# Seven products over all eight feature tiles in the second network's up projection

## The chip, the core and the metric

The kernel runs on one core of a Trainium2 chip. Its engines work side by side, each through its own fixed list of instructions: TensorE (PE, matmuls, with weight loads shown as PEld), VectorE (DVE), ScalarE (ACT), GpSimd (POOL) and SyncE (SP). Here POOL does nothing but issue DMAs, and SP issues most of the others. Matmuls write to PSUM, everything else lies in SBUF. An instruction waits on semaphores until its inputs are written and its output buffer is free, and everything behind it on the same engine waits too. The metric is the device time of one execution in microseconds.

## The reference, cut to what matters

A two-layer backbone (a state-space mixer, then differential attention), each layer followed by a gated convolutional network on 640 tokens (512 latent, 128 context), width 1024. The change touches that network, for the most part that of the second layer:

```python
def conv_ffn(h, up_w, conv_w, conv_b, down_w):
    u = dwconv(h @ up_w, conv_w, conv_b)
    a, v = jnp.split(u, 2, axis=-1)
    return (jax.nn.silu(a) * v) @ down_w
...
xs = xs + s_g2 * conv_ffn(modulate(xs, norm_ffn_g[i], s_sh2, s_sc2), *ffn_p)
```

`up_w` is 1024 x 5632, `down_w` is 2816 x 1024. All is float32.

## The kernel before, in words

**Precision.** Each operand of a large matmul is split into a high part (rounded by an ACT copy to the format that TensorE reads, `fp32r`) and a low part (what is left). A product is three matmuls: high x high, high weight x low data, low weight x high data (`block`, line 652; `dense_many`, line 184). `cast` (line 134) makes both parts of a weight: ACT the high part, DVE the low part by a subtraction (line 171). For weights in `self.summed` (line 1380) the low part is made otherwise (lines 167 and 168): ACT writes the negated high part, and a DMA issued by POOL adds the original weight from DRAM onto it.

**Weights.** `weight_units` (line 1343) lists all weights in order. `prefetch` loads them into four `raw` buffers, `cast` into high and low buffers: a pool `w` of three and, in the networks, a pool `x` of two, chosen by the unit's number (line 143). A new weight takes the buffer of the one that many places back in its pool, so its cast waits until PE is done with that one.

**The network** (`ffn`, line 627). The hidden width is 22 tiles of 128. A "pair" p is the gate tile p and the value tile p, each a 128-row slice of the up product. `epilogue` (line 639) turns a pair into a gated tile: convolution of both halves (`conv`: one ACT step, then steps on DVE), SiLU on ACT, product on DVE, then its high part `mh` (ACT) and low part `ml` (DVE). After a portion of the pairs, `project_out` (line 308) multiplies their gated tiles with the down weights: eight output tiles, each added to the residual by three DVE operations (`gate_add`). `SUB` gives three portions of 8, 7 and 7 pairs; one more pair than the portion holds is done before its projection. `start_tiles` (line 342) does the first three up tiles in two halves of the tokens, the first half while the second half of `h` is still being normalised.

**Seven products.** From pair `S0[l]` on (16 in the first network, 4 in the second) four of the eight feature tiles are handled as a 2 x 2 block product: rows are the gate and the value weights, the inner dimension two groups of `NS` = 2 feature tiles, columns the two halves of the tokens (320 each). `pair7` (line 701) forms it by seven block products instead of eight, with sums of weights (`s12`, `s34`, made by DVE in `cast`) and sums of data (`T1` to `T4`, made once by `operands`, line 663, in a round per feature tile while earlier pairs run). The other four feature tiles (`rest`) are multiplied in the ordinary way, 4 x 4 weight tiles.

**Order.** The program is written in one sequence; a scheduler places each engine's instructions by priority and its own estimate of time, and that order is then fixed for each engine.

Of the kernel before, what the change touches and what calls it, by code (L numbers as in the profile page):

```python
# [18 lines left out]
P = 128  # L19
# [29 lines left out]
class Step:  # L49


    def __init__(self, ctx, tc, a):
        self.ctx, self.tc, self.nc, self.a = ctx, tc, tc.nc, a
        self.tasks = []
        self.ticks = 0
        self.wi = 0
        self.normt = {}
        self.ready = []
        self.px = None
        self.modtask = None  # L60
        self.late = []
        self.down = False
        self.wraw, self.wcast = {}, {}
        self.units = []
# [57 lines left out]
    def prefetch(self, upto):  # L122
        while len(self.wraw) <= min(upto, len(self.units) - 1):
            u = len(self.wraw)
            ap, n = self.units[u]
            if ap is None:
                self.wraw[u] = None
                continue
            r = self.pw.tile([P, 1024], F32, tag="raw", name=f"raw{u}", bufs=RAW)
            dst = r[:, :n]  # L130
            self.nc.sync.dma_start(dst.rearrange("p (i c) -> p i c", i=ap.shape[1]) if len(ap.shape) == 3 else dst, ap)
            self.wraw[u] = r

    def cast(self, upto):
        while len(self.wcast) <= min(upto, len(self.units) - 1):
# [1 line left out]
            self.prefetch(u)  # L137
            n = self.units[u][1]
            r = self.wraw[u]
            sums = self.units[u][0] is None  # L140
            c0 = 2 * NS * P if u and self.units[u - 1][0] is None else 0
            wp, t, b = (self.pw, "w", 3) if self.px is None or u % 5 < 3 else (self.px, "x", 2)
            hi = wp.tile([P, 1024], F32R, tag=t + "hi", name=f"whi{u}", bufs=b)
            lo = wp.tile([P, 1024], F32R, tag=t + "lo", name=f"wlo{u}", bufs=b) if u else None
            if u == 0:
# [4 lines left out]
            elif sums:  # L150
                self.prefetch(u + 1)
                ra, rv = self.wraw[u - 1], self.wraw[u + 1]
                w = NS * P
                s12, s34 = (self.slot("f", nm, bufs=NF) for nm in ("s12", "s34"))
                self.tt(s12[:, :w], rv[:, :w], rv[:, w:2 * w], ALU.add)
                self.tt(s12[:, w:2 * w], s12[:, :w], ra[:, :w], ALU.subtract)
                self.tt(s34[:, :w], ra[:, :w], rv[:, :w], ALU.subtract)
                self.tt(s34[:, w:2 * w], ra[:, w:2 * w], s12[:, w:2 * w], ALU.subtract)
                for j, s in enumerate((s12, s34)):
                    c = slice(2 * w * j, 2 * w * (j + 1))  # L160
                    self.act(hi[:, c], s[:, :2 * w], AF.Copy)
                    self.tt(lo[:, c], s[:, :2 * w], hi[:, c].bitcast(F32), ALU.subtract)
            else:
                c = slice(c0 // 2, n)
# [462 lines left out]
    def ffn(self, l, h, nextnorm, pool):  # L627
# [11 lines left out]
        def epilogue(p, ua, uv):  # L639
# [6 lines left out]
            hi = self.slot("mh", f"mh{p}", F32R, bufs=9, pool=pool)  # L646
            lo = self.slot("ml", f"ml{p}", F32R, bufs=9, pool=pool)
            self.act(hi, cv, AF.Copy)
            self.tt(lo, cv, hi.bitcast(F32), ALU.subtract)
            mid[p] = (hi, lo)  # L650

        def block(ps, w, c0, xs, first, last, more=False):

            hi, lo = w
            for i, (xh, xl) in enumerate(xs):
# [4 lines left out]
                if i % 2:  # L660
                    self.hook()

        def operands(out):

            cut = lambda t, j: t[:, j * TH:(j + 1) * TH]
            B = [[[tuple(cut(t, j) for t in h[NS * k + i]) for i in range(NS)] for j in range(2)] for k in range(2)]
            Ts = [[], [], [], []]
            for i in range(NS):
                f1, f2 = self.tmp("f1"), self.tmp("f2")
                for f, k in ((f1, i), (f2, NS + i)):  # L670
# [7 lines left out]
                yield 4  # L678
                if l:
                    hi, lo = (pool.tile([P, 3 * TH], F32R, tag=f"T{nm}{i}", name=f"T{nm}{i}", bufs=1) for nm in "hl")  # L680
                elif i:
                    both = pool.tile([P, 2, 3 * TH], F32R, tag="cbc", name=f"T{i}", bufs=1)
                    hi, lo = both[:, 0, :], both[:, 1, :]
                else:
                    hi, lo = (pool.tile([P, 3 * TH], F32R, tag="mw", name=f"T{nm}{i}", bufs=2) for nm in "hl")
                t3 = self.slot("f", f"T3_{i}", F32R, bufs=NF)
                for o, x in ((slice(0, T), t12), (slice(T, T + TH), cut(t43, 0))):
# [3 lines left out]
                self.act(cut(t3, 0), cut(t43, 1), AF.Copy)  # L691
                self.tt(cut(t3, 1), cut(t43, 1), cut(t3, 0).bitcast(F32), ALU.subtract)
                Ts[0].append((cut(hi, 0), cut(lo, 0)))
                Ts[1].append((cut(hi, 1), cut(lo, 1)))
                Ts[2].append((cut(t3, 0), cut(t3, 1)))
                Ts[3].append((cut(hi, 2), cut(lo, 2)))
                yield 3
            rest = [[tuple(cut(t, j) for t in h[k]) for k in range(2 * NS, KT)] for j in range(2)]
            out.extend((B, Ts, rest))

        def pair7(p, B, Ts, rest):


            (B11, _), (B21, B22) = B
# [1 line left out]
            u = self.wi  # L706
            self.wi += 3
            self.prefetch(u + 6)
            self.cast(u + 3 if l else u + 2)
            wa, ws, wv = (self.wcast[u + j] for j in range(3))  # L710
            w, r0 = NS * P, 2 * NS * P
            ua, uv = (self.slot("f", "uraw", bufs=NF) for _ in range(2))
            p5 = self.slot("f", "p5", bufs=NF)[:, :TH]
            lft, rgt = slice(0, TH), slice(TH, T)
            ps = self.dense_ps("up")
            X, Y = ps[:, :TH], ps[:, 512:512 + TH]
            block(X, wa, 0, B11, True, True)
# [26 lines left out]
                self.act(uv[:, lft], X, AF.Copy)  # L744
            epilogue(p, ua, uv)

        def pair(p):
            if p >= S0[l]:
                self.drain(self.seven)
                return pair7(p, *sevens)  # L750
# [5 lines left out]
        sevens = []  # L756
        self.seven = self.add(operands(sevens), 8) if l else None
        for s, (k0, k1) in enumerate(SUB):
            self.down = False
            while done < min(k1 + 1, FT):  # L760
                pair(done)
# [5 lines left out]
            if s == len(SUB) - 1 and self.modtask:  # L767
                self.drain(self.modtask)
            if s < len(SUB) - 1:
# [573 lines left out]
    def weight_units(self):  # L1343
# [9 lines left out]
        def ffn(l):  # L1353
            done = 0
            out = []
            for k0, k1 in SUB:
                while done < min(k1 + 1, FT):
                    sums = [(None, 1024)] if done >= S0[l] else []
                    out.extend([(a["w_up"][l, done], 1024), *sums, (a["w_up"][l, FT + done], 1024)])
                    done += 1  # L1360
                out.extend([(a["w_dn"][l, i, :, k0 * P:k1 * P], (k1 - k0) * P) for i in range(KT)])
            return out

        u += ffn(0)
# [8 lines left out]
        u += ffn(1)  # L1373
        return u
# [138 lines left out]
```

## Time and profile before

| | |
|---|---|
| median of 3 runs | 1866.02 us (1863.74 to 1867.49) |
| profiled execution | 1866.73 us, of which the span from first to last instruction is 1865.0 |
| mean granted TensorE clock | 0.994 |
| second network | from about 1391 us to the end |
| its first seven-product pair (pair 4) | at 1449.5 us |

A page of the profile gives busy times per engine, the chain of work that ended last (followed back from the last instruction to what released each step), and groups of equal instructions. In a group's row, `out<-in` names what is written and read; behind the bar stand the busy time and the mean duration, then the idle time of the engine just before these instructions and what ended it. A timeline row gives start and duration in us. Instructions on DVE and ACT overlap a little, so the distance from start to start is shorter than the duration.

### The profile page before, as it was taken

Reading aid. Unit: us, or ns where it says so; the run is one execution under the profiler, and the core shown is the slowest. Engines: PE = TensorE matmul, PEld = TensorE weight load, DVE = VectorE, ACT = ScalarE, POOL = GpSimd, SP = SyncE. Lnnn points to the kernel's source line nnn. Section 1 sums busy time; section 2 is a strip of 40 time slices with the busy share of each in tenths; the row PEclk is TensorE's granted clock in tenths of the full one; section 3 lists DMA queues with packets and bytes.
Section 4 is the critical chain, followed back from the end, with each engine's and each line's share of the span. In section 5 each row is a group of like instructions: output and inputs, shape, how many; then the busy total and the mean of one; then the engine's idle time right before and its main releaser. Section 6 shows DMA issues by size and latency. Waiting matters only on the chain.

```text
span 1865.0 us, 33040 instructions
## 1 busy us (share of the span) xinstructions
PE 1822.6 (98%) x13178; PEld 1720.5 (92%) x13178; DVE 1447.5 (78%) x2877; ACT 1005.3 (54%) x1889; POOL 31.7 (2%) x40
## 2 busy tenths in 40 slices
PE   7999999999999999999999999999999999999997
PEld 5899999989999999999999988888899999999996
DVE  5689999999758999986685878778878772772774
ACT  3489687878336441442453556567547642652751
POOL 0000000000000000000000000000000000100100
PEclk9999999999999999999999999999999999999998
DMA  9845343436533556532131211111122552653531
GB/s 333 262 133 141 100 151 100 134 123 198 185 113 117 193 178 220 190 111 74 50 110 61 89 51 64 59 42 51 53 100 59 130 141 66 160 138 79 138 98 57
DMA packets 84866, 226.28 MB, mean 121 GB/s; under 512 B 9852, under 2 KB 16616, under 8 KB 84584
## 3 DMA queue, kind: packets, MB, share of 16 engines
q1 hardware_dynamic: 78952, 207.13, 34.2%
q0 software_dynamic: 5184, 16.52, 5.0%
q8 instruction: 103, 1.69, 0.4%
q10 hardware_dynamic: 576, 0.52, 0.1%
q14 instruction: 51, 0.42, 0.1%
HBM read 218.18 MB, written 5.96 MB: 120 GB/s over the span
## 4 chain that ended last, share of the span: by engine, by line
PE 88%; DVE 5%; ACT 3%; DMA 2%; issue 1%; SPq 0%; DVEq 0%; ACTq 0%
PE up L107 30%; PE po L107 25%; PE z L107 6%; PE x L107 5%; PE st L107 5%; PE bc L107 3%; PE yp L107 3%; PE q L107 2%; PE k L107 1%; PE modrow L107 1%; PE sl L107 1%; PE in L107 1%; ACT whi L98 1%; ACT e L98 1%; PE ov L107 1%
## 5 line engine op out<-in xcount | busy, mean ns | idle before, releaser
L98 ACT ACTIVATE whi<-raw 128x1024 fp32r<-128x1024 f32 (+3 forms) x227 | 228.5, 1008 | 297.3 <-PE po L107 175.5
L104 DVE TENSOR_TENSOR wlo<-raw,whi 128x1024 fp32r<-128x1024 f32 (+2 forms) x190 | 224.2, 1181 | 46.5 <-ACT whi L98 41.3
L101 DVE SCALAR_TENSOR_TENSOR xr<-po,mod,xr 128x256 f32<-128x256 f32 (+2 forms) x231 | 89.6, 435 | 149.9 <-PE po L107 149.7
L107 PE MATMUL po<-mh,whi 128*128 128x256 f32 (+1 forms) x704 | 168.1, 310 | 0.1
L107 PE MATMUL po<-ml,whi 128*128 128x256 f32 (+1 forms) x704 | 167.6, 310 | 0.0
L107 PE MATMUL po<-mh,wlo 128*128 128x256 f32 (+1 forms) x704 | 167.2, 309 | 0.0
L107 PE MATMUL up<-h01h,whi 128*128 128x256 f32 (+1 forms) x596 | 147.2, 310 | 0.1
L107 PE MATMUL up<-h01l,whi 128*128 128x256 f32 (+1 forms) x596 | 146.3, 308 | 0.0
L107 PE MATMUL up<-h01h,wlo 128*128 128x256 f32 (+1 forms) x596 | 145.7, 308 | 0.0
L107 PE MATMUL up<-h11h,whi 128*128 128x320 f32 (+1 forms) x476 | 141.6, 313 | 1.5 <-ACT uraw L98 1.2
L107 PE MATMUL up<-h11l,whi 128*128 128x320 f32 (+1 forms) x476 | 140.1, 308 | 0.0
L107 PE MATMUL up<-h11h,wlo 128*128 128x320 f32 (+1 forms) x476 | 137.9, 308 | 0.0
L107 PEld LDWEIGHTS po<-mh,whi 128*128 128x128 f32 x704 | 128.4, 188 | 0.8 <-ACT mh L98 0.5
L107 PEld LDWEIGHTS po<-ml,whi 128*128 128x128 f32 x704 | 128.5, 188 | 0.2 <-DVE ml L104 0.2
L107 PEld LDWEIGHTS po<-mh,wlo 128*128 128x128 f32 x704 | 128.5, 188 | 0.0
L107 PEld LDWEIGHTS up<-h01h,whi 128*128 128x128 f32 x596 | 109.1, 188 | 1.7 <-ACT uraw L98 1.2
L107 PEld LDWEIGHTS up<-h01l,whi 128*128 128x128 f32 x596 | 109.2, 188 | 0.0
L107 PEld LDWEIGHTS up<-h01h,wlo 128*128 128x128 f32 x596 | 109.0, 188 | 0.0
L101 DVE SCALAR_TENSOR_TENSOR cv<-uraw,fcw,cv 128x511 f32<-128x511 f32 (+1 forms) x176 | 86.8, 549 | 24.1 <-ACT cv L98 23.9
L107 PEld LDWEIGHTS up<-h11h,whi 128*128 128x128 f32 x476 | 88.7, 188 | 5.2 <-ACT uraw L98 2.9
L101 DVE SCALAR_TENSOR_TENSOR ca<-uraw,fcw,ca 128x511 f32<-128x511 f32 (+1 forms) x176 | 90.4, 550 | 2.8 <-ACT ca L98 2.0
L107 PEld LDWEIGHTS up<-h11l,whi 128*128 128x128 f32 x476 | 88.9, 188 | 0.0
(527 smaller groups left out, 4845.3 us busy)
## 6 DMA issues: line engine op xcount, KB each, us to landing
raw<-in_w_up SPq DMA_DIRECT2D x88, 512.0 KB, 3.7
mw<-in_modT SPq DMA_DIRECT2D x48, 512.0 KB, 4.0
raw<-in_w_in SPq DMA_DIRECT2D x40, 512.0 KB, 5.3
rb<-rowd SPq DMA_DIRECT2D x40, 512.0 KB, 5.6
raw<-in_w_dn SPq DMA_DIRECT2D x32, 448.0 KB, 3.3
raw<-in_w_qkv SPq DMA_DIRECT2D x24, 512.0 KB, 3.3
mr<-in_mod SPq DMA_DIRECT2D x44, 256.0 KB, 5.3
wlo<-in_w_up POOLq DMA_DIRECT2D x18, 512.0 KB, 7.2
```

Of the source, the lines that this page charges most:

```text
L98: return self.nc.scalar.activation(out, in_, func, **k)
L101: return self.nc.vector.scalar_tensor_tensor(out, in0, s, in1, op0, op1)
L104: return self.nc.vector.tensor_tensor(out, a, b, op)
L107: return self.nc.tensor.matmul(out, lhsT, rhs, start=start, stop=stop, skip_group_check=more)
```

## The change

In the second network the 2 x 2 block product covers all eight feature tiles: `NS` becomes 2 and 4, so a pair there is seven block products of four feature tiles and no rest. The pair has four weight units (gate, `s12`, `s34`, value); the gate always takes pool `x`, the other three pool `w`. The new `pair8` and `begin7` run a pair, the first product of the next pair ahead of the last of this one. `operands` makes four rounds there; the data of `T4` overwrite the second half of the first four tiles of `h`, in `finish_operands`, when pair 4 is reached. The down projection has five portions (4, 4, 4, 4 and 6 pairs), with six buffers for gated tiles in place of nine. The low parts of the gated tiles, all but the last, are made by a negated ACT copy and an accumulating DMA from POOL's queue (a copy within SBUF), and the low parts of all 44 up weights of the second network by such a DMA, where before it was those of pairs 4 and after. In the first network the sums of weights are cast one by one, and `T4` is finished last.

```diff
-SUB = ((0, 8), (8, 15), (15, 22))
+SUB = ((0, 8), (8, 15), (15, 22)), ((0, 4), (4, 8), (8, 12), (12, 16), (16, 22))
+MIDS = 9, 6
-NS = 2
+NS = 2, 4
...
-            sums = self.units[u][0] is None
-            c0 = 2 * NS * P if u and self.units[u - 1][0] is None else 0
-            wp, t, b = (self.pw, "w", 3) if self.px is None or u % 5 < 3 else (self.px, "x", 2)
+            kind = self.units[u][2]
+            place = self.units[u][3] or ("x" if self.px and u % 5 > 2 else "w")
+            wp, t, b = (self.pw, "w", 3) if place == "w" else (self.px, "x", 2)
...
+            elif isinstance(kind, tuple):
+                ns, j0, ia, iv = kind
+                self.prefetch(u + iv)
+                ra, rv = self.wraw[u + ia], self.wraw[u + iv]
+                w = ns * P
+                for j in range(j0, j0 + 1024 // w):
+                    x = self.slot("f", f"s{j}", bufs=NF)[:, :w]
+                    a, b, op = ((rv[:, :w], rv[:, w:2 * w], ALU.add), (self.s.get(0), ra[:, :w], ALU.subtract),
+                                (ra[:, :w], rv[:, :w], ALU.subtract), (ra[:, w:2 * w], self.s.get(1), ALU.subtract))[j]
+                    self.tt(x, a, b, op)
+                    self.s[j] = x
+                    c = slice(w * (j - j0), w * (j - j0 + 1))
+                    self.act(hi[:, c], x, AF.Copy)
+                    self.tt(lo[:, c], x, hi[:, c].bitcast(F32), ALU.subtract)
...
             self.act(hi, cv, AF.Copy)
-            self.tt(lo, cv, hi.bitcast(F32), ALU.subtract)
+            if l and p < FT - 1:
+                self.act(lo, cv, AF.Copy, scale=-1.0)
+                nc.gpsimd.dma_start(lo, cv, accum_op=ALU.add)
+            else:
+                self.tt(lo, cv, hi.bitcast(F32), ALU.subtract)
...
                 if l:
                     hi, lo = (pool.tile([P, 3 * TH], F32R, tag=f"T{nm}{i}", name=f"T{nm}{i}", bufs=1) for nm in "hl")
+                    x4 = tuple(cut(t, 1) for t in h[i])
+                    late.append((x4, cut(t43, 0)))
+                    parts = (slice(0, T), t12), (slice(T, T + TH), cut(t43, 1))
...
+        def begin7(p):
+            u = self.wi
+            self.wi += 4
+            self.prefetch(u + 7)
+            self.cast(u + 2)
+            ua, uv = (self.slot("f", "uraw", bufs=NF) for _ in range(2))
+            if self.nps % 2:
+                Y, X, V = bank(), bank(), bank()
+            else:
+                X, V, Y = bank(), bank(), bank()
+            (B11, _), _ = sevens[0]
+            block(X, self.wcast[u], 0, B11, True, True)
+            with self.tc.high_priority():
+                self.act(ua[:, lft], X, AF.Copy)
+            self.cast(u + 3)
+            return u, ua, uv, X, Y, V
+
+        def pair8(p, more):
+            u, ua, uv, X, Y, V = self.began or begin7(p)
...
+            block(V, s12, 0, T1, True, True)
+            with self.tc.high_priority():
+                self.act(p5, V, AF.Copy)
+            self.cast(u + 4)
+            block(X, s12, w, T2, False, True, True)
+            with self.tc.high_priority():
+                self.act(ua[:, rgt], X, AF.Copy)
+            block(V, s34, w, B22, False, True, True)
+            with self.tc.high_priority():
+                self.tt(ua[:, rgt], V, ua[:, rgt], ALU.add)
+            if more:
+                self.cast(u + 5)
+            block(X, s34, 0, T3, False, True, True)
+            with self.tc.high_priority():
+                self.tt(uv[:, rgt], X, p5, ALU.add)
+            block(Y, wa, w, B21, True, True)
+            with self.tc.high_priority():
+                self.tt(ua[:, lft], Y, ua[:, lft], ALU.add)
+            self.began = begin7(p + 1) if more else None
+            block(X, wv, w, T4, False, True, True)
+            with self.tc.high_priority():
+                self.act(uv[:, lft], X, AF.Copy)
+            if not more:
+                self.nps += self.nps % 2
+            epilogue(p, ua, uv)
...
+        def finish_operands():
+            for (hi, lo), x in sevens[3]:
+                self.act(hi, x, AF.Copy)
+                self.tt(lo, x, hi.bitcast(F32), ALU.subtract)
...
-        sums = [u for u, (ap, _) in enumerate(self.units) if ap is None]
-        self.summed = {u + j for u in sums[-18:] for j in (-1, 1)}
+        last = [u for u, x in enumerate(self.units) if x[0] is not None and x[0].name == a["w_up"].name][-2 * FT:]
+        self.summed = set(last)
```

More of the change, by code (lines that the diff above doesn't have):

```diff
@@ L149, in cast @@
                 self.tt(half(hi, 1), r3, half(hi, 0).bitcast(F32), ALU.subtract)
[L150 to L162, printed above, removed]
+            elif isinstance(kind, tuple):
[12 more added lines that the diff above has]
+                    self.tt(lo[:, c], x, hi[:, c].bitcast(F32), ALU.subtract)
             else:
-                c = slice(c0 // 2, n)
+                c = slice(kind or 0, n)
                 self.act(hi[:, c], r[:, c], AF.Copy)
@@ L699, in operands, with bank @@
-            out.extend((B, Ts, rest))
-        def pair7(p, B, Ts, rest):
+                for j in range(3):
+                    Ts[j].append((cut(hi, j), cut(lo, j)))
+                Ts[3].append(x4)
+                yield 3
+            rest = [[tuple(cut(t, j) for t in h[k]) for k in range(2 * ns, KT)] for j in range(2)]
+            out.extend((B, Ts, rest, late))
+        def bank():
+            if self.nps % 2 == 0:
+                self.pst = self.dense_ps("up")
+            self.nps += 1
+            return self.pst[:, (self.nps - 1) % 2 * 512:][:, :TH]
@@ new lines, in pair8 @@
+        def pair8(p, more):
+            u, ua, uv, X, Y, V = self.began or begin7(p)
+            (_, _), (B21, B22) = sevens[0]
+            T1, T2, T3, T4 = sevens[1]
+            wa, s12, s34, wv = (self.wcast[u + j] for j in range(4))
+            w = ns * P
+            p5 = self.slot("f", "p5", bufs=NF)[:, :TH]
+            block(V, s12, 0, T1, True, True)
[23 more added lines that the diff above has]
+            epilogue(p, ua, uv)
@@ L756, in ffn @@
         sevens = []
+        self.began = None
         self.seven = self.add(operands(sevens), 8) if l else None
-        for s, (k0, k1) in enumerate(SUB):
+        for s, (k0, k1) in enumerate(SUB[l]):
             self.down = False
             while done < min(k1 + 1, FT):
-                pair(done)
+                pair(done, done + 1 < min(k1 + 1, FT))
                 done += 1
@@ L1355, in ffn @@
             out = []
-            for k0, k1 in SUB:
+            ns = NS[l]
+            m = ns * 4 * P // 1024
+            for k0, k1 in SUB[l]:
                 while done < min(k1 + 1, FT):
-                    sums = [(None, 1024)] if done >= S0[l] else []
-                    out.extend([(a["w_up"][l, done], 1024), *sums, (a["w_up"][l, FT + done], 1024)])
+                    seven = done >= S0[l]
+                    pl = ("x", "w") if seven and l else (None, None)
+                    sums = [(None, 1024, (ns, j * 4 // m, -1 - j, m - j), pl[1]) for j in range(m)] if seven else []
+                    out.extend([(a["w_up"][l, done], 1024, None, pl[0]), *sums,
+                                (a["w_up"][l, FT + done], 1024, ns * P if seven else None, pl[1])])
                     done += 1
-                out.extend([(a["w_dn"][l, i, :, k0 * P:k1 * P], (k1 - k0) * P) for i in range(KT)])
+                out.extend([(a["w_dn"][l, i, :, k0 * P:k1 * P], (k1 - k0) * P, None, None) for i in range(KT)])
             return out
-        u += ffn(0)
+        u = [(*x, None, None) for x in u] + ffn(0)
+        v, u = u, []
         for hd in range(8):
```

63 lines of the change are left out of this document (33 added, 30 removed).

## The prediction

> **What bounds the kernel now.** I read the page first: span, busy shares, then the chain of work that ended last.
>
> ```profile
> span 1865.0 us, 33040 instructions
> PE 1822.6 (98%) x13178; PEld 1720.5 (92%) x13178; DVE 1447.5 (78%) x2877; ACT 1005.3 (54%) x1889; POOL 31.7 (2%) x40
> ...
> PE 88%; DVE 5%; ACT 3%; DMA 2%; issue 1%; SPq 0%; DVEq 0%; ACTq 0%
> PE up L107 30%; PE po L107 25%; PE z L107 6%; PE x L107 5%; PE st L107 5%; PE bc L107 3%; PE yp L107 3%; PE q L107 2%; PE k L107 1%; PE modrow L107 1%; PE sl L107 1%; PE in L107 1%; ACT whi L98 1%; ACT e L98 1%; PE ov L107 1%
> ```
>
> TensorE sets the end: 88% of the chain is matmuls, and up products (`up`) and down projections (`po`) are over half of it. The change lies in the second network, so next I read the busy time of each engine in its stretches: its four ordinary pairs, the turn to the seven products, and stretches of pairs 4 and after.
>
> ```profile
> 1414.50:1449.60 35.10, 35.10 (x241) 35.10 (x240) 30.64 (x58) 24.82 (x34) 2.73 (x3) 1.00 0.34 79
> ...
> 1420.00:1460.00 40.00, 38.51 (x261) 37.99 (x261) 30.77 (x57) 23.40 (x35) 2.73 (x3) 1.00 0.36 89
> ...
> 1466.00:1506.00 40.00, 40.00 (x273) 39.66 (x272) 30.58 (x63) 26.87 (x43) 5.06 (x6) 1.00 0.66 151
> 1574.00:1667.00 93.00, 93.00 (x627) 91.61 (x626) 68.24 (x135) 57.75 (x91) 9.57 (x11) 1.00 0.57 134
> ```
>
> The columns are length, then PE, weight load, DVE, ACT, POOL (busy us and count), granted clock, DMA share, GB/s. In the pairs PE is never idle, at full granted clock, and VectorE has a quarter of its time free. So a matmul left out is time saved, and any wait that reaches PE is time lost. The one gap, 1.5 us, lies at the turn (1420 to 1460). A 320-column matmul costs 40.00/273 = 0.1465 us.
>
> **The gain.** A seven-product pair takes 7x2 + 4x4 = 30 weight tiles of three matmuls, 90 in all; over eight feature tiles it takes 7x4 = 28, so 84. Six fewer in each of 18 pairs: 108 x 0.1465 = 15.8 us, a pair falling from 13.2 to 12.3 us. The down projections keep their 22x8 weight tiles, whether in three portions or five, so PE pays nothing for the split. Now each wait that this brings.
>
> **Can VectorE and ScalarE keep up within a pair?** The rows of operations added and removed (count | busy us, mean ns):
>
> ```profile
> L104 DVE TENSOR_TENSOR wlo<-s,whi 128x512 fp32r<-128x512 f32 x36 | 24.3, 689 | 5.3 <-ACT whi L98 5.2
> ...
> L104 DVE TENSOR_TENSOR ml<-cv,mh 128x640 fp32r<-128x640 f32 x20 | 16.5, 825 | 12.2 <-ACT mh L98 12.2
> ...
> L104 DVE TENSOR_TENSOR uraw<-up,p 128x320 f32<-128x320 f32 x18 | 8.8, 488 | 5.7 <-PE up L107 5.7
> L104 DVE TENSOR_TENSOR s<-raw,s 128x256 f32<-128x256 f32 x18 | 7.6, 421 | 0.1
> ...
> L98 ACT ACTIVATE whi<-s 128x512 fp32r<-128x512 f32 x36 | 21.6, 618 | 9.2 <-PE po L107 9.2
> ...
> L98 ACT ACTIVATE mh<-cv 128x640 fp32r<-128x640 f32 x20 | 14.8, 739 | 42.9 <-DVE cv L104 42.9
> L98 ACT ACTIVATE whi<-raw 128x768 fp32r<-128x768 f32 x17 | 14.2, 838 | 28.3 <-PE up L107 17.1 <-issue 11.1
> ```
>
> The 93 us stretch holds 93/13.2 = 7.05 pairs: 9.7 us of DVE and 8.2 us of ACT each. DVE gains four sums of 512 columns for four of 256 (4 x 0.27 = 1.1) and two more low parts (1.4), and loses the gated tile's low part (0.83) and one output add (0.49): 10.8 of 12.3 us. ACT gains two high parts (1.24) and the negated gated tile (0.74), and saves 2 x 0.22 on the shorter value weights: 9.7 of 12.3. With the first pair's weights cast during the projection, a group of four needs the casts of three, which leaves about 20% free. Bounds 0 to 6 us over the net; I take 1.5, nearest to the full PE of now.
>
> ```profile
> L101 DVE SCALAR_TENSOR_TENSOR xr<-po,mod,xr 128x256 f32<-128x256 f32 (+2 forms) x231 | 89.6, 435 | 149.9 <-PE po L107 149.7
> ```
>
> Two projections more are 16 tiles x 3 such gate adds, 48 x 0.435 = 21 us of DVE, in stretches where DVE waits for PE (149.7 us in this row): hidden, and worth at most those 21 us if DVE entered the projections late.
>
> **Accumulating DMAs.** A low part now is: ACT high part, ACT negated copy, DMA that adds the original. It replaces one DVE subtraction for the gated tiles and for the eight weights of pairs 0 to 3. The landing times after issue on POOL's queue, alone and beside loads, and the ACT copies one after the other:
>
> ```profile
> wlo<-in_w_up POOLq DMA_DIRECT2D x1, 384.0 KB, 4.4
> ...
> wlo<-in_w_up POOLq DMA_DIRECT2D x1, 512.0 KB, 5.2
> ...
> wlo<-in_w_up POOLq DMA_DIRECT2D x1, 512.0 KB, 7.6
> ...
> DMA to landing us min/median/max: 4.4/6.9/8.5
> ```
>
> ```profile
> 1390.64 1.04 ACT L98 ACTIVATE whi<-raw 128x1024 fp32r<-128x1024 f32 x1
> 1391.59 0.49 ACT L98 ACTIVATE h11h<-nt,mod 128x256 fp32r<-128x256 f32 x1
> 1391.98 1.04 ACT L98 ACTIVATE whi<-raw 128x1024 fp32r<-128x1024 f32 x1
> ```
>
> So from a free buffer to a usable 1024-column low part it takes 2 x 0.95 + 5.2 to 7.6 = 7.1 to 9.5 us (DVE's subtraction follows the high part at once). Where that shows, by the changed program's order of instructions:
>
> Start of the network: the second weight's buffer comes free when attention's projection ends, at 1390.64, where the row above casts it. High part to 1391.6, the last `h11h` of the first half (0.4), negated copy to 1392.95, landed at 1398.2 to 1400.6. PE has the first weight's half, then four matmuls that need high parts alone, then stands:
>
> ```profile
> 1394.99 4.03 PE st L107 x32
> ```
>
> It gets there at about 1396.3 (the first weight's last seven matmuls, then those four, at 4.03/32 = 0.126): 1.9 to 4.3 us lost, plus up to 1 for the third weight behind it. I take 3.0. The norm's broadcast (`nbc`) is queued behind this wait on PE, and with it the second half of `h`.
>
> Pair 5, the first after a projection: its gate weight is fixed to the two-buffer pool `x`, and takes the buffer of down weight 6 of 8. After that tile PE has one tile (24 matmuls) and six high-part matmuls: 30 x 0.147 = 4.4 us. Lost: 2.7 to 5.1; I take 3.5. Pair 10 takes the buffer of the last down weight, 50 matmuls (7.3 us) ahead: 0 to 2.2, taken 1.1. The other groups' weights find buffers freed 74 or more matmuls (10.9 us) ahead: nothing.
>
> Ends of groups: from the last-but-one pair's last block, copy 0.42, conv, product, high part, negated copy and landing make some 10 to 14 us, against 81 matmuls (11.9 us) until the projection needs its last low part. 0 to 2 us at four places, taken 3.0 together.
>
> **The turn at pair 4.** This is the largest term. The operands now take four rounds instead of two on DVE, and DVE's order in the changed program puts the convolution of pair 3's value half ahead of the last round and a half. That convolution waits for the last ordinary tile, exactly when PE turns to pair 4, which has 24 matmuls of plain tiles and two high-part ones to do (3.8 us) before it needs the first low part of a sum. From the trace:
>
> ```profile
> 1449.66 0.70 ACT L98 ACTIVATE uraw<-up 128x640 f32<-128x640 f32 x1 [1.71 <-PE up L107]
> 1450.40 0.92 ACT L98 ACTIVATE cv<-uraw,fcw 128x640 f32<-128x640 f32 x1
> ```
>
> ```profile
> 1426.81 0.82 DVE L104 TENSOR_TENSOR f<-h11h,h11l 128x640 f32<-128x640 f32 x1
> 1427.55 0.82 DVE L104 TENSOR_TENSOR cv<-ca,cv 128x640 f32<-128x640 f32 x1
> 1428.28 0.49 DVE L104 TENSOR_TENSOR t<-f,t 128x320 f32<-128x320 f32 x1
> 1428.68 0.48 DVE L104 TENSOR_TENSOR t<-f,f 128x320 f32<-128x320 f32 x1
> ...
> 1451.35 1.94 DVE L101 SCALAR_TENSOR_TENSOR cv<-uraw,fcw,cv 128x511 f32<-128x511 f32 x4 [2.77 <-ACT cv L98]
> 1453.20 0.69 DVE L104 TENSOR_TENSOR wlo<-s,whi 128x512 fp32r<-128x512 f32 x1
> 1453.80 0.82 DVE L104 TENSOR_TENSOR cv<-ca,cv 128x640 f32<-128x640 f32 x1
> ```
>
> From tile end to convolution 1451.35 - 1449.66 = 1.7. Start to start, the convolution's four steps are 1.85, a 640-column operation 0.74, one of 320 columns 0.40, one of 512 columns 0.60. Behind the convolution DVE has four of 640 (product, a low part, a feature sum, a low part: 2.96), nine of 320 (3.6), two sums and one down weight's low part (1.8), then the low part itself (0.69): 10.9. In all 12.6, against 3.8: 8.8 us of stall in place of 1.5. Net 7.3. Nearly every item has its own row, so the bounds are narrow: 6, to 11 where DVE comes late to the convolution because scratch buffers are held by the gated tiles' DMAs.
>
> **Sum.** -15.8 + 3.0 + 7.3 + 3.5 + 1.1 + 3.0 + 1.5 = +3.6 us. The profiled execution took 1866.73 us (span 1865.0), 0.7 above the median of the runs, 1866.02: forecast 1870.3.
>
> The Trainium skill, DMA: Bandwidth & Descriptors, section "Anatomy of one DMA", fits such a transfer as 2.0 us plus bytes over 436 GB/s, an estimate of 3.2 us for 512 KB. The rows above, 5.2 to 7.6, disagree for this accumulating kind. By the page the waits at the start and at the groups' ends vanish, pair 5's shrinks to 0.7 and the sum is -6.3, 1860.4: the side of the first rival.
>
> **Rivals.**
> Faster, landings hidden: they come at the low end and the groups' ends are covered. For: alone they took 4.4 to 5.2. Against: the DMA share in pairs is 0.66 now. All lower bounds: -15.8 + 1.9 + 6 + 2.7 = -5.2, so 1861.5. Chance 0.24.
> Faster, the turn hidden too, if DVE passes it as it does now: -15.8 + 6 = 1857. Against: the added list is counted. Chance 0.06.
> Slower, the pair's own bound moves to DVE and ACT: at 10.8 and 9.7 of 12.3 us, in fixed orders that wait for each other, the pair stays at 13.2. It decides once their waits exceed 1.5 us in a pair. 13 pairs x 0.9 = 11.7: 1882. For: DVE waited 5.7 us for the `up`-and-`p` adds already. Chance 0.15.
> Slower, the DMA engines:
>
> ```profile
> q0 software_dynamic: 5184, 16.52, 5.0%
> ```
>
> Accumulates take 0.050 x 1865/16.52 = 5.6 us per MB, and a pair now sends 1.11 MB (gate 512, value 256, gated tile 320 KB): 6.3 us of 12.3, beside loads. The next gate weight's buffer is freed 84 matmuls ahead; over 10.4 us of landing it is late. At 11.4, 13 pairs x 1 = 13: 1883. Chance 0.08.
> That the change does not do what it says is out: the program has 108 matmuls fewer.
>
> **How the numbers follow.** Forecast, stalls a little above the gain: 0.47, own range 1866 to 1876. From 0.2% (3.7 us, what a measurement can tell) on, it is slower in 0.29, level in 0.17, faster in 0.01. The first rival is 0.21 faster, 0.03 level; the second faster; the other two slower. Faster 0.28, same 0.20, slower 0.52. The range reaches to 1859 and 1882; outside lie most of the second rival and part of the slow ones.
>
> **What would show it.** In the profile after: PE idle of 7 to 10 us between the plain blocks of pair 4 and its first `Th` block, with DVE busy; PE idle of 2 to 5 us in `st` and at the first pair after the first projection, ended by a DMA; no idle inside later pairs, which take 12.3 us. A pair of 13 us with DVE above 90% makes the third rival right; gate weights' DMAs landing after 10 us, the fourth; no idle at the turn, the second, and my largest term wrong.

## The result, and the profile after

| kernel | median us | lowest to highest | ratio to the kernel before, 95% interval |
|---|---|---|---|
| before | 1866.76 | 1863.74 to 1867.62 (4 runs) | 1 |
| changed | 1888.61 | 1886.57 to 1892.66 (4 runs) | 1.0123, 1.010 to 1.0145 |

The change makes the kernel 21.9 us slower; the forecast was 4.3 slower. The profiled execution of the changed kernel took 1892.66 us, the longest of its four, so its spans show some 4 us more than the median has. One execution of three_waits_out below, 1970.5 us at a granted clock of 0.848 where the other four have 0.995, is left aside throughout. First the page:

```profile
span 1889.8 us, 33199 instructions
PE 1821.7 (96%) x13070; PEld 1712.8 (91%) x13070; DVE 1480.2 (78%) x2960; ACT 1049.0 (56%) x1988; POOL 57.1 (3%) x69
...
q0 software_dynamic: 9360, 25.24, 7.7%
...
PE 7%; DVE 1%; ACT 0%; DMA 0%; issue 0%; DVEq 0%; ACTq 0%
```

The 108 matmuls are gone (13178 to 13070), yet PE is busy as long as before (1822.6 then): a matmul of now is longer somewhere. PE idles 68.1 us instead of 42.4. The chain of waits covers only the last 8% of the span, so the stages have to be read from windows. Busy time by stage of the changed kernel, from the second network's first product on (four ordinary pairs; pair 4 and the first projection; groups two, three and four; group five to the end), and under it the first of these stages in the kernel before. Columns: window, length, PE, weight load, DVE, ACT, POOL, granted clock, DMA share, GB/s:

```profile
1388.03:1454.49 66.46, 60.88 (x425) 59.63 (x425) 44.10 (x103) 41.14 (x63) 7.87 (x9) 0.97 0.52 112
1454.49:1512.92 58.43, 46.64 (x277) 45.43 (x277) 36.16 (x73) 24.65 (x41) 4.35 (x5) 0.82 0.34 90
1512.92:1600.70 87.78, 81.36 (x529) 78.69 (x529) 57.01 (x112) 46.54 (x77) 10.49 (x12) 0.98 0.55 130
1600.70:1681.30 80.60, 79.28 (x531) 77.41 (x530) 57.28 (x112) 47.67 (x77) 10.49 (x12) 1.00 0.59 136
1681.30:1761.90 80.60, 79.83 (x530) 77.54 (x529) 57.12 (x112) 46.80 (x77) 10.48 (x12) 1.00 0.57 134
1761.90:1889.80 127.90, 111.75 (x789) 108.03 (x787) 82.50 (x170) 58.74 (x100) 10.45 (x12) 0.95 0.40 99
```

```profile
1390.64:1449.46 58.82, 58.82 (x425) 57.98 (x425) 49.91 (x109) 37.66 (x59) 2.73 (x3) 1.00 0.28 74
```

The start holds the same 425 matmuls in both kernels and takes 7.6 us more. Pair 4 (12.3) and a projection of four tiles (28.0, a window of an experiment below) should take 40.3 and take 58.4: 18.1 lost, with a granted clock of 0.82. A group of four pairs and a projection should take 4 x 12.3 + 28.0 = 77.2; the second takes 87.8, the third and fourth 80.6 each. So there are three places that lose much, and 3.4 us in every later full group (of these PE idles 0.8 to 1.3 us; the rest stands in its busy time). What PE waited for, from 1380 to 1890 (engine, what ended the wait: us in total, times, longest):

```profile
PE up L110 <- ACT uraw L101: 11.8, 3, 10.8
PE st L110 <- DMA wlo<-in_w_up: 5.6, 2, 4.6
PE up L110 <- DMA wlo<-in_w_up: 3.9, 1, 3.9
PE up L110 <- ACT p L101: 3.2, 4, 0.9
...
PE po L110 <- ACT whi L101: 1.3, 2, 0.8
...
PE po L110 <- DMA ml<-cv: 0.6, 1, 0.6
```

**The turn**, on PE and then on DVE and ACT (start, length, instruction, in brackets the wait before it):

```profile
1457.87 0.30 PE L110 MATMUL up<-h11h,wlo 128*128 128x320 f32 x1
1468.93 0.64 PE L110 MATMUL up<-Th,whi 128*128 128x320 f32 x1 [10.76 <-ACT uraw L101]
1469.37 0.47 PE L110 MATMUL up<-Tl,whi 128*128 128x320 f32 x1
```

```profile
1456.39 1.93 DVE L104 SCALAR_TENSOR_TENSOR cv<-uraw,fcw,cv 128x511 f32<-128x511 f32 x4 [2.36 <-ACT cv L101]
...
1464.80 0.68 DVE L107 TENSOR_TENSOR s<-raw 128x512 f32<-128x512 f32 x1
...
1466.61 0.68 DVE L107 TENSOR_TENSOR wlo<-s,whi 128x512 fp32r<-128x512 f32 x1
```

```profile
1454.69 0.71 ACT L101 ACTIVATE uraw<-up 128x640 f32<-128x640 f32 x1 [2.57 <-PE up L110]
...
1467.92 0.63 ACT L101 ACTIVATE whi<-s 128x512 fp32r<-128x512 f32 x1 [0.57 <-DVE s L107]
1468.46 0.42 ACT L101 ACTIVATE uraw<-up 128x320 f32<-128x320 f32 x1
```

The last ordinary tile is copied at 1454.69, its convolution starts 1.7 us later, and from there to the end of the first sums' low part (1467.29) DVE works 10.9 us without a pause. ACT's copy of the first block's result stands behind the casts of the sums in ACT's order and costs PE 1.6 us more. Then the clock, in stretches of 5 us (last three columns: granted clock, DMA share, GB/s):

```profile
1460.00:1465.00 5.00, 0.00 (x0) 0.00 (x0) 5.00 (x12) 2.46 (x5) 0.87 (x1) 0.59 0.37 66
1465.00:1470.00 5.00, 1.07 (x4) 1.07 (x5) 5.00 (x9) 3.34 (x7) 0.00 (x0) 0.50 0.19 52
1470.00:1475.00 5.00, 4.47 (x17) 4.07 (x16) 0.70 (x2) 0.87 (x2) 0.87 (x1) 0.50 0.74 157
1475.00:1480.00 5.00, 4.50 (x17) 4.10 (x17) 0.69 (x1) 0.95 (x2) 0.00 (x0) 0.50 0.19 52
1480.00:1485.00 5.00, 5.00 (x31) 4.87 (x30) 2.48 (x5) 1.56 (x2) 0.00 (x0) 0.86 0.00 0
```

While PE stands, the granted clock falls to 0.50, and it stays there after PE has resumed: 17 matmuls in 5 us, where 34 would fit, until 1482. Start to start a 320-column matmul is 0.267 us instead of 0.1465. PE resumed at 1468.93; of the 13.1 us to 1482.07 it waited 1.0 and lost 12.1 x (1 - 0.1465/0.267) = 5.5 us by the clock.

**The start and pair 5**, on PE, and the transfers that they wait for, on POOL:

```profile
1399.00 0.38 PE L110 MATMUL st<-h11h,wlo 128*128 128x256 f32 x1 [4.64 <-DMA wlo<-in_w_up]
...
1518.83 0.60 PE L110 MATMUL up<-h11h,wlo 128*128 128x320 f32 x1 [3.90 <-DMA wlo<-in_w_up]
```

```profile
1390.35 0.89 POOL L172 DMA_DIRECT2D wlo<-in_w_up  x1 [4.62 <-ACT wlo L101]
...
1511.77 0.87 POOL L172 DMA_DIRECT2D wlo<-in_w_up  x1 [3.50 <-ACT wlo L101]
```

Issued at 1390.35, the start's transfer of 512 KB releases PE at 1399.0, after 8.6 us; pair 5's, issued at 1511.77, at 1518.8, after 7.0. Behind both stops the matmuls are half as fast for 3.7 and 3.4 us, by the spacing of their starts: 1.6 and 1.5 us more. In the profiled execution the half clock costs 5.5 + 1.6 + 1.5 = 8.6 us in all.

### The profile page after: what moved, and what is told of

It reads as the page before. It is cut to its first block, busy times and chain, and to the rows that moved or that the text cites. A ratio compares the mean times of both kernels' runs of the same rounds, so it can differ in the third digit from the quotient of the medians.

```text
span 1889.8 us, 33199 instructions
## 1 busy us (share of the span) xinstructions
PE 1821.7 (96%) x13070; PEld 1712.8 (91%) x13070; DVE 1480.2 (78%) x2960; ACT 1049.0 (56%) x1988; POOL 57.1 (3%) x69
## 5 line engine op out<-in xcount | busy, mean ns | idle before, releaser
L107 DVE TENSOR_TENSOR wlo<-raw,whi 128x1024 fp32r<-128x1024 f32 (+3 forms) x198 | 215.7, 1092 | 53.0 <-ACT whi L101 45.5
L104 DVE SCALAR_TENSOR_TENSOR xr<-po,mod,xr 128x256 f32<-128x256 f32 (+2 forms) x279 | 107.7, 432 | 112.9 <-PE po L110 112.7
L110 PE MATMUL up<-h11h,whi 128*128 128x320 f32 (+1 forms) x368 | 109.4, 318 | 2.8 <-ACT uraw L101 1.1
L110 PE MATMUL up<-h11h,wlo 128*128 128x320 f32 (+1 forms) x368 | 107.6, 313 | 3.9 <-DMA wlo<-in_w_up 3.9
L104 DVE SCALAR_TENSOR_TENSOR ca<-uraw,fcw,ca 128x511 f32<-128x511 f32 (+1 forms) x176 | 87.8, 545 | 28.6 <-ACT ca L101 28.6
L110 PE MATMUL up<-h11l,whi 128*128 128x320 f32 (+1 forms) x368 | 107.9, 311 | 0.0
L104 DVE SCALAR_TENSOR_TENSOR cv<-uraw,fcw,cv 128x511 f32<-128x511 f32 (+1 forms) x176 | 85.8, 545 | 14.9 <-ACT cv L101 14.9
L110 PE MATMUL up<-Th,whi 128*128 128x320 f32 x234 | 76.9, 329 | 14.1 <-ACT uraw L101 10.8
L172 POOL DMA_DIRECT2D wlo<-in_w_up x44 | 38.5, 875 | 1633.5 <-ACT sq L101 1375.3
```

What stands on the lines that cost most here:

```text
L104: return self.nc.vector.scalar_tensor_tensor(out, in0, s, in1, op0, op1)
L107: return self.nc.vector.tensor_tensor(out, a, b, op)
L110: return self.nc.tensor.matmul(out, lhsT, rhs, start=start, stop=stop, skip_group_check=more)
```

## The experiments

All are the changed kernel (1888.6 us) with the edit shown, unless said otherwise; none leaves work out. "Waits" are PE's between 1380 and the end.

### The start's low parts on DVE (start_dve)

```
-        self.summed = set(last)
+        self.summed = set(last[2 * S0[1]:])
```

> The low parts of the first eight up weights of the second network (its four ordinary pairs) are made on DVE again, all else as in the changed kernel (1888.6 us). Theory of the waits: the stage from the first product of the network to the end of its ordinary pairs, 66.5 us in the changed kernel, falls to about 59; -7.5, so 1881 (1879 to 1884), and no PE wait over 1 us is left in st. Rival, load: DVE gets 8 x 1.1 = 9 us more before the turn, the operands come later and the turn's wait grows by most of what the start gains: 1886 to 1889.

Measured: 1880.6 us, ratio 1.0078 (1.0058 to 1.0097), 8.0 below the changed kernel. Its waits have no row for `st` any more, and the rest is as it was:

```profile
PE up L110 <- ACT uraw L101: 11.8, 3, 10.8
PE up L110 <- DMA wlo<-in_w_up: 4.4, 1, 4.4
...
```

The eight subtractions do not lengthen the turn (10.8 as before). The rival, load, falls for this stage.

### Pair 4 the ordinary way (turn_hidden)

```
-S0 = 16, 4
+S0 = 16, 5
```

> One pair more, pair 4, is computed the ordinary way, so that the first projection (28 us of matmuls) stands between the last ordinary pair and the first seven-product pair. Theory of the waits: the 18 us that the stretch from pair 4 to pair 5 loses go, against 1.7 us for the twelve matmuls' worth of work that pair 4 costs more; the wait at pair 5's gate weight (about 7 us with its half clock) moves to a later group, because the buffers are dealt out otherwise: 1872 (1869 to 1877). Rival, load: DVE is late with the operands and sums in any case, and the wait only moves to pair 5: 1883 or more.

Measured: 1878.8 us, ratio 1.0065 (1.005 to 1.008): -9.8 instead of -17.

```profile
PE up L110 <- DMA wlo<-in_w_up: 5.7, 2, 3.0
PE st L110 <- DMA wlo<-in_w_up: 5.3, 2, 4.5
...
```

The row of 10.8 us is gone, so the projection hides the whole chain on DVE. But the buffers are dealt by a weight's running number, which shifts by two here, and now two later groups wait for their gate weight (2.7 and 3.0, each with half clock behind it; these two groups take 4.6 and 5.7 us longer than in the changed kernel), where I had counted one. The direction was right, the expected size was not.

### The turn's wait filled (turn_filled)

```
+            if p == S0[l]:
+                (B11, _), _ = sevens[0]
+                for _ in range(FILL):
+                    self.mm(Y, wa[0][:, :P], B11[0][0], True, True)
             block(V, s12, 0, T1, True, True)
```

> 66 products of no use (320 columns, into a PSUM bank that is overwritten afterwards) are put before the first block of the first seven-product pair, 66 x 0.1465 = 9.7 us of the 10.8 us for which PE waits there. Theory, clock: the wait itself stays, but PE never idles long enough for its clock to fall, and the 46 matmuls behind it are 0.147 us apart instead of 0.27: -5.8 us, 1883 (1881 to 1885). Rival: the half clock is no consequence of the idle time (the evacuations or the DMAs of this stretch slow the matmuls): 1888 or a little more.

Measured: 1888.4 us, ratio 1.0114 (1.0097 to 1.0131): no gain. In the trace the matmuls after the fill are 0.147 us apart, and from the first sum block to pair 5 it is 39.1 us instead of 44.0. But the first sum block came 82.0 us after the network's start instead of 80.9, because two of ACT's casts had moved ahead of the copy that releases it. Behind the start and pair 5 the half clock lasts 1.8 and 1.3 us longer after PE's resuming than in the changed kernel's trace. And the profiled execution of the changed kernel, against which I had set 5.8, is its longest. So this run shows that idle time brings the half clock, and leaves its size in a typical run open; it was tried again below with ACT's order nearly kept.

### The gate weight's buffer (gate_buffer)

```
+DN = "wxwxwwww"
...
-        (k1 - k0) * P, None, None) for i in range(KT)])
+        (k1 - k0) * P, None, DN[i] if l else None) for i in range(KT)])
```

> The buffers of the down weights are dealt out by place in the projection, so that the first gate weight of every group takes a buffer that is freed five tiles before the projection's end; its low part still comes by accumulating DMA. Theory of the waits: the stop of 4.6 us at pair 5 and the half clock behind it (1.7) go, with 0.9 us around them: -7, 1881.5 (1880 to 1884). Rival, DMA: the low part lands late because the transfer is slow or waits in its queue, wherever its buffer is: 1886 to 1889.

Measured: 1882.7 us, ratio 1.0093 (1.007 to 1.0115): -5.9. No wait of `up` for a low part is left in its list. The transfer is as it was, only its buffer is free earlier: the wait was for the buffer.

### Gated tiles on DVE (gated_dve)

```
-            if l and p < FT - 1:
-                self.act(lo, cv, AF.Copy, scale=-1.0)
-                nc.gpsimd.dma_start(lo, cv, accum_op=ALU.add)
-            else:
-                self.tt(lo, cv, hi.bitcast(F32), ALU.subtract)
+            self.tt(lo, cv, hi.bitcast(F32), ALU.subtract)
```

> The low parts of the gated tiles are DVE's subtraction again (0.83 us each on DVE, and no negated copy of 0.72 on ACT and no DMA), all else as in the changed kernel (1888.6 us). Theory of the waits: PE waits for these DMAs only 0.6 us in all in the changed kernel, so this part costs nothing: 1886 to 1890. Rival, the prediction's term for the ends of groups (landings of gated tiles, 3.0) and its rival of the DMA engines: 1885.5 or less.

Measured: 1889.4 us, ratio 1.0126 (1.0111 to 1.0142). By itself this part of the change does nothing either way.

### Five projections in the kernel before (five_before)

```
-SUB = ((0, 8), (8, 15), (15, 22))
+SUB = ((0, 8), (8, 15), (15, 22)), ((0, 4), (4, 8), (8, 12), (12, 16), (16, 22))
```

> The kernel before with five down projections in its second network (the changed kernel's cut), nothing else. Theory: the 3 us and more that every later group of the changed kernel loses come from its own order at a group's last pair (no next pair's blocks between its own), not from there being five projections: 0 to +3 on the kernel before, 1866 to 1869. Rival: a further group costs 3.3 us whatever the pairs look like: +6.6, 1873.

Measured: 1866.8 us over ten runs, ratio 1.000 (0.9991 to 1.0009). Splitting the projections is free. The later groups' 3.4 us belong to the new pairs.

### The three repairs together, and the ends (three_waits_out, ends_filled, ends_gated_dve)

The first has the edits of start_dve, turn_hidden and gate_buffer; as the cut follows `S0`, ten low parts are on DVE there. The second adds this to it:

```
-DN = "wxwxwwww"
+DN = "xwwxwwww"
...
+            if not more:
+                self.cast(u + 4)
             block(V, s12, 0, T1, True, True)
```

The third adds the edit of gated_dve.

> The changed kernel with the three repairs together: first eight low parts on DVE, pair 4 ordinary, down weights' buffers by place. Theory of the waits: start -8, turn -18 + 1.7, gate weights' waits -7: 1860 (1857 to 1864), below the kernel before, with 13 pairs of 84 matmuls at 12.3 us plus the groups' ends. Rival, load: DVE and ACT are the bound once the waits are gone, and the gains do not add: 1868 or more.

> As the kernel with the three repairs, and the first down weight of each projection goes into the other pool, whose buffer is free early, and is cast one block earlier, so that its products can stand between the first two sum blocks of a group's last pair, where PE waits 1.1 and then 0.7 us now. Theory of the ends: 5 x 1 to 1.5: -5, 1855 (1852 to 1858). Rival: the wait only moves to the gated tiles' landings behind it: the same time as without this edit.

> As ends_filled (1857.1), with the gated tiles' low parts by DVE's subtraction. Theory of the ends: the 2.9 us for which PE waits for the landing of gated tiles at the ends of groups go, -2 to -3: 1854.5. Rival, load: DVE's 0.83 us more in each pair come back as waits for sums and evacuations: 1857 or more.

Measured: 1858.9 (0.9958, 0.9944 to 0.9971), 1857.1 (0.9943, 0.9931 to 0.9956) and 1853.0 us (0.9924, 0.9910 to 0.9937). All three are faster than the kernel before. The waits of the three, one fence each:

```profile
PE up L111 <- ACT p L102: 3.8, 4, 0.9
PE po L111 <- ACT whi L102: 2.5, 4, 0.8
...
```

```profile
PE po L111 <- DMA ml<-cv: 2.9, 4, 0.9
...
```

```profile
PE nbc L111 <- DVE rs_y L105: 2.5, 1, 2.5
PE up L111 <- DVE uraw L108: 0.7, 2, 0.4
PE ms L111 <- ACT sq L102: 0.7, 1, 0.7
```

In a group's last pair there is no next pair whose blocks could stand between its own, so its second sum block waits for the copy of the first (`p`), and the first products of the projection wait for their weight. Casting that weight early fills both gaps, 6.3 us, but gives only 1.8 by the medians, and the two intervals overlap: the products that fill them now come to the gated tile of the pair before, whose transfer has not landed (2.9). The rival was largely right. With DVE's subtraction this wait goes too, -4.1 (-3.5 by the ratios; the intervals just overlap). So the gated tiles' part, free in the changed kernel, costs some 4 us once the rest is repaired. One projection and one group of the last kernel:

```profile
1459.70:1487.70 28.00, 28.00 (x194) 28.00 (x193) 20.49 (x43) 12.23 (x19) 1.88 (x2) 1.00 0.50 132
1487.70:1566.70 79.00, 79.00 (x531) 77.35 (x530) 59.91 (x116) 44.22 (x73) 6.98 (x8) 1.00 0.51 120
```

79.0 us, against 77.2 of products.

### The turn alone, and filled (turn_alone, turn_alone_filled)

start_dve (here `last[8:]`) and gate_buffer together, pair 4 as in the changed kernel; in the second, 60 products of no use as in turn_filled.

> The changed kernel with the first eight low parts on DVE and the down weights' buffers by place, but pair 4 as in the changed kernel, so that of its three stops only the turn is left. Theory: against the kernel with all three repairs (1858.9) it pays the turn's 18 us and saves the 1.7 of the ordinary pair 4: 1875, and its runs lie some 5 us apart, because the time for which the half clock lasts after a stop of 10.8 us differs from run to run. Rival, load: the turn is only where the lateness of DVE shows, and without the other stops in front it grows: 1880 or more.

> As turn_alone, with 60 products of no use (8.8 us) in the turn's wait; the order on DVE is the same and on ACT only one copy moves by a place. Theory, clock: the part of the turn that is half clock goes, 2 to 6 us, and with it most of the spread between runs: 1871 (1869 to 1873), within 2 us of each other or little more. Rival: filling the wait changes the clock in the records and not the time (as turn_filled seemed to say): 1875 with the same spread.

Measured: 1873.1 us (1870.1 to 1879.4; ratio 1.0036, 1.0024 to 1.0048) and 1872.3 (1869.7 to 1875.6; 1.0024, 1.0014 to 1.0034). The intervals overlap. The first came out near the 1875 that was expected, not at its rival's 1880; the second lies in its range, but its runs lie 5.9 us apart, not 2. In stretches of 5 us, first of turn_alone (PE resumes at 1458.8 after 10.7 us), then of the filled one (it resumes at 1460.8 after 1.9 us):

```profile
1460.00:1465.00 5.00, 4.38 (x21) 3.71 (x20) 1.19 (x2) 1.22 (x3) 0.00 (x0) 0.78 0.76 194
1465.00:1470.00 5.00, 4.47 (x29) 4.32 (x30) 1.63 (x3) 1.72 (x3) 0.00 (x0) 1.00 0.19 52
```

```profile
1460.00:1465.00 5.00, 3.68 (x16) 3.28 (x17) 2.85 (x5) 2.33 (x5) 0.87 (x1) 0.71 0.64 153
1465.00:1470.00 5.00, 4.50 (x18) 4.10 (x17) 0.76 (x2) 0.95 (x2) 0.00 (x0) 0.50 0.31 70
```

In this execution of turn_alone the half clock lasted 3.4 us after PE resumed, in the changed kernel's 12.4; and the filled kernel, with a wait of only 1.9, fell to it 1.3 us after resuming and stayed there for 10. The last section shows why.

Both profiled executions are ends of their series: that of turn_alone has the lowest of its ten times, that of the filled kernel the second highest of its twelve. The granted clock, which is known for every run, tells more. In turn_alone it goes from 0.994 (1870.05 us) to 0.989 (1879.37): 0.005 x 1870 = 9.4 us of clock, where the times differ by 9.3. So the spread of its times is, nearly all of it, the half clock. With the fill the clock is 0.994 to 0.996 in ten runs, and 0.992 and 0.993 in the other two, which have the highest times (1875.5 and 1875.6). PE reaches the first sum block 73.2 us after the network's start in both profiles, so the fill delays nothing. It keeps the clock in most runs, then, but with 2 us of wait left open not in all.

The 5.5 us of the changed kernel's profile are one draw, though by the granted clock not an extreme one (0.988; the other three runs have 0.986, 0.989 and 0.990). What the half clock costs at the turn in a typical run stays open within bounds: the fill gains 0.8 us by the medians and 2.2 by the ratios; and the whole turn, 15.9 us (14.4 in the table below, plus the 1.5 that the kernel before lost), leaves 4.0 beyond the stop of 10.7 and the two short waits of 0.5 and 0.6 behind it.

## Why the prediction was wrong

The gain and the places of the large stalls were right; nearly every stall was sized too small. By its own terms, in us, measured by medians:

| term of the sum | predicted | measured | from |
|---|---|---|---|
| 108 matmuls fewer | -15.8 | -15.8 | counts; full groups run at 0.1465 |
| start | +3.0 | +8.0 | start_dve |
| turn at pair 4 | +7.3 | +14.4 | turn_alone - three_waits_out = 14.2, + 1.7 for the ordinary pair 4 there, - 1.5 that the kernel before lost too |
| gate weights of pairs 5 and 10 | +4.6 | +5.9 | gate_buffer |
| ends of groups and load in the pairs | +4.5 | +7.9 | three_waits_out gains 7.7 of 15.6 |
| sum | +3.6 | +20.4 | 21.9 measured as a whole |

The 15.6 in the fifth row: 17 pairs x 6 x 0.1465 = 14.9, less 0.8 for the ordinary pair 4 against one of 90 products (14.0 - 13.2), plus the old turn's 1.5. By the ratios in place of the medians no row moves by 1 us. The fifth row is what the other rows leave over. By the traces it is larger: the second network takes 470.1 us in three_waits_out and 474.3 in the kernel before, 4.2 of 15.6 gained, so 11.4 lost, and three groups there take 80.9, 80.7 and 80.9 us against 77.2 of products (10.9 in sum). The difference lies ahead of the second network, which begins anywhere from 1385.6 to 1393.2 us in these traces. With either figure the single terms come within 2 us of the whole, so the stops are nearly independent.

**The gain** stands. The rival of a pair that stays at 13.2 us for want of DVE and ACT is refuted: start_dve gave DVE more work at the start and lost nothing, ends_gated_dve has DVE at 59.9 of 79 us in a group and comes within 2 us of its products. The rival of the DMA engines did not show either: behind pair 5 no `up` product of the changed kernel waited for the transfer of a gate weight.

**The turn.** The step was right to a tenth in what it listed: 1.7 us to the convolution and 10.9 behind it, as predicted. Its cover was 3.5 us rather than 3.8. It failed in two things. It followed DVE alone: ACT's copy of the first block waits behind casts that wait for DVE, 1.6 us more. And it ended the cost at the moment when PE resumes, while PE then ran at half clock, and two short waits of 0.5 us came behind it. The range of 6 to 11 called narrow did not hold it.

**The start.** The place and the two waits were right. The landing took 8.6 us after issue, beyond the 5.2 to 7.6 that I carried over from the kernel before, where transfers are alone or beside loads; the prediction's own row of all such transfers went to 8.5. Here four such transfers and the loads meet:

```profile
wlo<-in_w_up POOLq DMA_DIRECT2D x4, 512.0 KB, 8.5
```

(transfers issued between 1380 and 1400, KB each, median us to landing; the DMA share in the row below is 0.99).

```profile
1390.00:1400.00 10.00, 5.36 (x61) 4.32 (x61) 2.27 (x9) 2.71 (x4) 1.76 (x2) 0.97 0.99 234
```

The first weight's low part, which I had not counted, cost 1.0 (5.6 - 4.6 in the row of `st`), the half clock 1.6. The page of the Trainium skill that the prediction weighed (DMA: Bandwidth & Descriptors, section "Anatomy of one DMA", an estimate of 3.2 us) is further off: the trace disagrees with it for this kind of transfer.

**Pair 5** lost 7.2 in the profile (87.8 - 80.6) and 5.9 by medians, against 3.5; the wait itself was 3.9, so the mechanism and its first size were right, and the half clock (1.5) and the small waits around the stop (1.8) are what was missing. **Pair 10** waited for nothing.

**Ends of groups.** The term was there for the wrong reason: PE waited for gated tiles' landings 0.6 us, not 3.0. The loss came from the last pair's own copies, `p` and the projection's first weight, with no next pair to fill the gaps. The prediction followed a pair in the middle of a group, where the next pair's blocks lie between, and counted for the last one only its gated tiles.

**The common fault** has two parts. A stop was taken to cost its own length. The Trainium skill has the rule that speaks against this (TensorE: Matmul & The Clock Gate, section "Part 1: The HAM clock gate (the "warmup" mystery)"): an idle stretch of about 3.4 us halves PE's clock, and as much steady work is needed to bring it back. The stops of 4.6 and 3.9 us here agree, with 3.7 and 3.4 us of half clock behind them. In two things the traces differ: a wait of 1.9 us was enough in turn_alone_filled, and behind the turn short waits of 0.5 us drew the half clock out to 12.4 us (last section). And the cases were not laid out evenly: the first rival put all stalls at their lower bounds together, but no case put them all at their upper bounds. That would have been -15.8 + 5.3 + 11 + 5.1 + 2.2 + 8 + 6 = +21.8, 1888.5. It would have met the measured 1888.6 by luck: the start and the turn went 2.7 and 3.4 us beyond their upper bounds, and the 14 us for ends and load stood against 7.9 (11.4 by the traces).

## What to carry to other kernels

Where an engine is always busy, work taken from it was gained here in full, but each place where it now stands must be priced with what follows: the clock behind the stop, the copies queued behind late casts on another engine, the transfers that meet there. Read the order of instructions at the first and the last pass of a loop, not only in its middle: nearly all the losses here lay there, and the repairs were a few lines each. When several costs have the same cause, put them at their high ends together once, and see whether the range still holds.

## What the hardware showed that I had not expected

The half clock after a stop is not of one length. Counted from PE's resuming, it lasted 3.7 and 3.4 us after stops of 4.6 and 3.9, but 3.4 us in one execution and 12.4 in another after the same stop of 10.7, and 10 us after a wait of 1.9.

The granted clock in the traces shows what fixes the length. It changes only on a grid of steps of 3.41 us. Every stretch of half clock is a whole number of steps long (3.41, 6.83, 10.24, 17.07 or 20.48 us), but for the one that the end of the program cuts off, and the stretches of one trace begin whole steps apart (1399.44, 1460.88 and 1518.91 in the changed kernel: 18 and 17 steps). This is PE's idle time in successive steps, with the steps at half clock in bold:

| trace, place | first step begins at | PE idle in each step, us |
|---|---|---|
| changed kernel, start | 1392.61 | 1.66, 2.98, **0.00**, then full clock |
| changed kernel, turn | 1457.47 | 2.71, **3.41**, **3.41**, **1.23**, **0.53**, **0.50**, **0.00**, then full clock |
| changed kernel, pair 5 | 1512.08 | 1.30, 3.34, **0.00**, then full clock |
| turn_alone, turn | 1448.58 | 3.41, **3.41**, **3.38**, **0.00**, then full clock |
| turn_alone_filled, turn | 1458.65 | 1.93, **0.53**, **0.50**, **0.00**, then full clock |

So the clock is halved behind a step with much idle time (1.93 us was enough, 1.66 was not), and it comes back behind a step in which PE never waits. Behind a step with a wait of 0.5 us it can stay down; in gated_dve and start_dve it came back behind such a step, so this lies near a border. The grid does not start with the stop, and so the same order of instructions meets it differently from execution to execution: in turn_alone PE resumed 0.04 us ahead of a step, which its first twelve products then filled; in the changed kernel it resumed 1.2 us into one, and its two short waits fell into the two steps behind it.

Not every difference between runs is the half clock: of the 21 runs of the kernel before beside turn_alone the lowest (1863.36 us) has a granted clock of 0.995 and the highest (1871.02) one of 0.993, 3.7 us of clock where the times differ by 7.7.

An accumulating transfer of 512 KB took 7.0 us to land at pair 5 and 8.6 at the start, the upper half of what the kernel before had shown and more.
